# Fourth queries with third values, fourth keys with fourth values: a regrouping of paired products in a streaming-encoder block

## The chip, the cores and the metric

The kernel runs on one core of a Trainium2 chip. The metric is device time in microseconds of one execution, the median of several runs. PE is the engine of matrix products, PEld its weight loads, DVE the vector engine, ACT the scalar engine, POOL the general engine and SP the queue that issues most transfers.

## What is computed

One layer of a block with two parallel branches, in float32, for 256 positions and a model width of 4096 (the reference, cut):

```python
xn = rms_norm(h, norm_in_g)
proj = xn @ w_in                      # 4096 x 14336
q, k, v, z_a, a_c, g_c, z_c = split(proj, 7 parts of 2048)
y_a = chunked_attention(q, k, v, rel_table)          # 16 heads of 128
y_a = rms_norm(y_a, attn_out_g) * silu(z_a)
y_c = conv_module(a_c, g_c, ...)  # a * sigmoid(g), 31-tap causal conv, layer norm, swish, @ w_pw
y_c = rms_norm(y_c, conv_out_g) * silu(z_c)
h = h + concat([y_a, y_c]) @ w_out
h = h + sigmoid(rms_norm(h) @ w_ple_gate + b) * (p @ w_ple)
out = rms_norm(h, final_g)
```

The change touches the part from `proj` to the layer norm of the convolution branch.

## The kernel before

**Exact products from parts.** Every float32 operand is split into a high and a low part: ACT copies the high part (`wh`, line 204), DVE subtracts it to get the low part (`wl`, line 205). A block product is three matmuls of 128x512 (high x high, low x high, high x low). The tags `wh` and `wl` have three tiles each, so the split can run at most three parts ahead of PE.

**Pairs of columns.** `mixed_product` multiplies x with two column blocks of 512 at once, for both halves of the 256 positions. It walks over 16 pairs of 128-row blocks in the order of a list. A plain pair does four block products for each of its two row blocks, 24 matmuls in all. A marked pair (`*` or `+`) does seven block products instead of eight, so 21 matmuls, at the price of sums of weight blocks: for `*` DVE makes four of them (lines 465, 466, 472, 473), for `+` two come ready from memory through an accumulating transfer issued on POOL (line 419) and DVE makes the other two. The sums are split as well (`uh`, `ul`). The combinations of x that a marked pair needs (`xS`) exist for pairs 0, 2, 4 and 6 from the start; for 8 and 10 they are made by `more_combinations` during one group.

Marked pairs need four more accumulators, the helpers P1, P5, P7 and P6. They take all four tiles of the pool of temporary PSUM banks (`ps_tmp`) from the first marked pair of a group to its last; attention, transposes and the matmuls of the layer norm use the same four banks at other times. After the last marked pair `on_helpers` reads them out.

A single product (`product`, line 229) has no marked pairs: 192 matmuls for one column block.

**Fills.** DVE work that is due later waits in the list `later`; after each pair of a group a few items are taken from it (`fill`, with counts such as `early_fills`). Items are the 124 taps of each of the four convolution groups (lines 717 and 721) and the 71 steps of `layer_norm_swish`: sums and mean (9 with pauses), centering and squares (20), variance, pauses, spread, pauses (10), 16 swishes and 16 splits into `uS`. The order on the engines is then settled by a scheduler that may move a ready instruction ahead of one that has to wait.

**Memory.** `upool` holds the sums of weights and their parts and some combinations of x; it is closed (`first_sums.close()`) when no marked pair of this part is left, and `more`, the pool of `uS`, is opened in its place. The tag `hd` has five tiles, for uT, biases, transposed keys, values, and the sum and squares of the layer norm.

**The order of groups** is written out by hand: convolution group 0 and 1; queries and keys 0; values 0 and 1 as a pair; attention 0; convolution group 2; queries and keys 1; attention 1; convolution group 3; queries and keys 2; values 2 alone; attention 2; layer norm put in the list; queries and keys 3, with `norm_fills`; `more` opened; values 3 alone; attention 3; then the pointwise product, which reads `uS`.

Of the kernel before, what the change touches and what calls it, by code (L numbers as in the profile page):

```python
# [10 lines left out]
F32 = mybir.dt.float32  # L11
F32R = mybir.dt.float32r
AF = mybir.ActivationFunctionType
# [3 lines left out]
P = 128  # L17
NB = 512
# [7 lines left out]
def hybrid_block(  # L26
# [23 lines left out]
    nc = tc.nc  # L50
# [131 lines left out]
    def fill(n):  # L182
        for _ in range(min(n, len(later))):
            later.popleft()()
# [139 lines left out]
    def units(text):  # L324

        return [(int(u.rstrip("*+")), u[-1] if u[-1] in "*+" else "") for u in text.split()]
# [2 lines left out]
    dense = units("1 0* 3 2* 5 4* 6* 7 8* 9 10* 11 12* 14* 13 15")  # L329
    first = units("0 1 3 5 7 9 11 13 15 2* 8 4* 10 6* 12 14")  # L330
    early = units("1 3 5 0+ 7 9 2+ 11 13 4+ 15 8 6+ 10 12 14")
    early_six = units("1 3 5 0+ 7 2* 9 4+ 11 6* 13 8+ 15 10* 12 14")

    early_fills = (5, 6, 1, 5, 6, 1, 5, 6, 1, 5, 6, 1, 2, 5, 5, 4)
    six_fills = (6, 6, 1, 5, 1, 5, 1, 5, 1, 5, 1, 5, 1, 6, 7, 7)
    norm_fills = (5, 5, 2, 5, 5, 2, 5, 5, 2, 5, 5, 2, 2, 4, 5, 5)
    final = units("1 0* 3 2* 5 4* 6* 7 8* 9 10* 12* 11 13 14 15")
    late = units("1 3 5 7 9 11 13 15 0* 2 4* 6 8* 10* 12 14")

    def mixed_product(  # L340
        w, col, lhs, comb, order, on_helpers, ahead=None, fills=(0,), on_begin=None, apart=NB,
        left=(), begin=None,
    ):


# [81 lines left out]
        for n, (pair, seven) in enumerate(order):  # L427
            if n < done:
                continue
            if ahead:  # L430
                ahead(pair)
            wts = []
            for k in range(2):
                wt = wpool.tile([P, 2, NB], F32, tag="w", name="wt")
                if seven == "+" and k == 0:
                    nc.sync.dma_start(wt[:, 0], w[2 * pair * P : (2 * pair + 1) * P, col : col + NB])
                else:
                    nc.sync.dma_start(wt, two_columns(w, 2 * pair + k, col, apart))
                wts.append(wt)
            sums_ahead(n)  # L440
            if n >= len(order) - n_left:
                for k in range(2):
                    tiles = left[2 * (n - len(order) + n_left) + k]
                    held.append((2 * pair + k, parts_of(wts[k], 2, tiles and tiles())[0]))
                fill(fills[n % len(fills)])
                continue
            if not seven:
                for k in range(2):
                    add_plain(n, k, *parts_of(wts[k], 2)[0])
                fill(fills[n % len(fills)])  # L450
                continue
            begins = not helper
            if begins:
                for name in ("P1", "P5", "P7", "P6"):
                    helper[name] = ps_tmp.tile([P, NB], F32, tag="tmp", name=f"acc_{name}")
                banks.update(helper)
            w0, w1 = wts
            plus = partial(nc.vector.tensor_tensor, op=ALU.add)
            before = list(recent)
            w0h, w0l = parts_of(w0, 1)[0]  # L460
            if seven == "+":
                ua = ub = sums[n]
            else:
                ua = ub = upool.tile([P, 2, NB], F32, tag="u", name="ua")
                plus(ua[:, 0], w0[:, 0], w0[:, 1])  # L465
                plus(ua[:, 1], w0[:, 1], w1[:, 1])  # L466
            with queued_behind(before if seven == "+" else ()):
                uah, ual = pair_parts(ua)
            w1h, w1l = parts_of(w1, 2)[0]
            if seven == "*" and not sums:  # L470
                ub = upool.tile([P, 2, NB], F32, tag="u", name="ub")
            plus(ub[:, 0], ua[:, 0], w1[:, 1])
            plus(ub[:, 1], ub[:, 0], w1[:, 0])  # L473
            ubh, ubl = pair_parts(ub)
            first = len(made)

            def s_of(i):
                t, at = comb[pair] if isinstance(comb, dict) else (comb[pair // 4], pair % 4)
                return [t[:, at + i // 2, q, (i % 2) * P : (i % 2 + 1) * P] for q in range(2)]

            k0, k1 = 2 * pair, 2 * pair + 1
            add("P1", block(k0, 0), (w0h[:, 0], w0l[:, 0]), n, True)
            add("P5", s_of(1), (uah[:, 0], ual[:, 0]), n, True)
            add("P7", s_of(0), (uah[:, 1], ual[:, 1]), n, True)
            add("P2", block(k1, 0), (w1h[:, 0], w1l[:, 0]), n, True)
            add("P3", s_of(3), (w1h[:, 1], w1l[:, 1]), n, True)
            add("P6", s_of(2), (ubh[:, 0], ubl[:, 0]), n, True)
            add("P4", block(k1, 1), (ubh[:, 1], ubl[:, 1]), n, True)
            if begins and on_begin:
                on_begin()  # L490
            if begins:
                tc.add_manual_dep(
                    made[first].ins, last_transpose[0].ins.name,
                    mybir.DependencyInfo(mybir.DependencyClass.NoSync, mybir.DependencyReason.DATA),
                    reason="transposes before the helpers take their banks",
                )
            if n == last_seven:
                on_helpers(helper)
            fill(fills[n % len(fills)])
        after.close()  # L500
        return (c, add_left) if left else c
# [10 lines left out]
        tt(z[1][0], helper["P7"], z[1][0], ALU.add)  # L512
        tt(z[1][1], helper["P5"], z[1][0], ALU.add)

    def sum_tiles(**kw):

        kw = kw or dict(tag="stage")
        t = [spool.tile([P, NH, NB], F32, name="z", **kw) for _ in range(2)]
        return t, [[t[j][:, h] for j in range(2)] for h in range(NH)]

    def scaled_pair(w, col, apart, order, r, fills, home={}, **kw):

        t, z = [], []

        def on_helpers(helper):
            for dst, src in zip((t, z), sum_tiles(**home)):
                dst.extend(src)
            nc.scalar.activation(z[0][0], helper["P1"], AF.Identity, scale=r[:, :1])
            helper_sums(helper, z)
            for h, j in QUARTERS[1:]:  # L530
                nc.scalar.activation(z[h][j], z[h][j], AF.Identity, scale=r[:, h : h + 1])

        c = mixed_product(w, col, xT, xS, order, on_helpers, fills=fills, apart=apart, **kw)
        for h, j in QUARTERS:
            stt(
                z[h][j], c[h][j], r[:, h : h + 1], z[h][j],
                ALU.mult, ALU.subtract if j else ALU.add,
            )
        return t
# [193 lines left out]
    def glu_conv(c):  # L733
        if c == 0:
            sg, gate = scaled_pair(
                w_in0, o_a, o_g - o_a, first, r_x, (1,), begin=first_pairs
            )
        else:
            last = c == CW // NB - 1
            sg, gate = scaled_pair(  # L740
                w_in0, o_a + c * NB, o_g - o_a, *((early_six, r_x, six_fills) if last else (early, r_x, early_fills)),
                ahead=more_combinations if last else None,
            )
        for h in range(NH):
            nc.scalar.activation(gate[:, h, :], gate[:, h, :], AF.Sigmoid)
# [193 lines left out]
        )  # L939
        nc.gpsimd.memset(bias[: P // 2, :, : P // 2], NEG)  # L940

    def keys(g, fills):
        q, k = scaled_pair(w_in0, o_q + g * NB, o_k - o_q, early, r_x, fills)
        qs[g] = act.tile([P, GH, T], F32, tag="act", name="qT")
        to_heads(q, qs[g])
        ks[g] = hd_tile("kT")
        to_heads(k, ks[g])

    def paired_values(g, order, fills, **kw):
        vs[g], vs[g + 1] = scaled_pair(w_in0, o_v + g * NB, NB, order, r_x, fills, **kw)  # L950

    def single_values(g):
        accv = product(w_in0, o_v + g * NB, xT, KD)
        vs[g] = spool.tile([P, NH, NB], F32, tag="hd", name="v", bufs=5)
        for h in range(NH):
            nc.scalar.activation(vs[g][:, h, :], accv[h], AF.Identity, scale=r_x[:, h : h + 1])

    n_g = H // GH
    assert n_g == CW // NB == 4
    glu_conv(0)  # L960
    glu_conv(1)
    load_bias(0)
    keys(0, early_fills)
    paired_values(0, early, early_fills, home=dict(tag="hd", bufs=5))
    attention(0)
    glu_conv(2)
    load_bias(1)
    keys(1, early_fills)
    attention(1)
    glu_conv(3)  # L970
    load_bias(2)
    keys(2, early_fills)
    single_values(2)
    attention(2)
    layer_norm_swish()
    load_bias(3)
    keys(3, norm_fills)
    first_sums.close()
    more = pool("more", 4)
    single_values(3)  # L980
    attention(3)
    r_a = rstd_of(ssq_a, AW, "r_a")

# [22 lines left out]
    for c0, order in zip(range(0, CW // NB, 2), point):  # L1006
# [7 lines left out]
        def on_helpers(helper):  # L1014
            y_tiles()
            z.extend([ys[j][:, h, :] for j in range(2)] for h in range(NH))
            tt(z[0][0], helper["P1"], rows[0], ALU.add)
            helper_sums(helper, z)
            for h, j in QUARTERS[1:]:
                tt(z[h][j], z[h][j], rows[j], ALU.subtract if j else ALU.add)  # L1020
# [318 lines left out]
```

## Time and profile before

| what | value |
|---|---|
| median of 3 runs | 2033.08 us (2032.29 to 2034.44) |
| the profiled execution | 2032.83 us |
| its span, first to last instruction | 2031.1 us |
| PE, DVE, ACT busy | 99%, 92%, 59% |
| granted TensorE clock | 0.998 |

A group row of the profile gives the line, the engine, the tiles written and read, the count, then busy time, the mean time of one in ns, and the idle time just before with what ended it. A row of the windows view gives a stretch, its length, and for each engine the busy time and the number of instructions, then the granted clock, the DMA engines' busy share and GB/s. Matmul durations overlap, so the spacing of matmuls is read from starts or from long runs, not from the duration of one.

### The profile page before, as it was taken

The page shows a single profiled execution, that of the slowest core. Times are in us where ns is not written, and L with a number is a line of the kernel's source. Part 1 is how long each engine was busy: PE and PEld are TensorE (multiplying, and loading weights), DVE is VectorE, ACT ScalarE, POOL GpSimd, SP SyncE. Part 2 cuts the span into 40 slices and gives each one's busy share as a digit, 9 for nine tenths or more (in the row PEclk, how much of TensorE's full clock was granted, in tenths as well). Part 3 has the DMA queues.
Part 4 walks back from the last instruction along what each step waited for, and adds up shares of the span by engine and source line. Part 5 has one row for each costly group of instructions (what it writes and reads, how often), then busy time and mean ns, then how long its engine had stood idle before and what let it go on. Part 6 is the DMA issues. An engine that isn't in the chain of part 4 may idle for free.

```text
span 2031.1 us, 26144 instructions
## 1 busy us (share of the span) xinstructions
PE 2015.5 (99%) x9094; PEld 1658.7 (82%) x9094; DVE 1871.1 (92%) x2658; ACT 1203.3 (59%) x1568; POOL 46.0 (2%) x50
## 2 busy tenths in 40 slices
PE   9999999999999999999999999999999999999997
PEld 7888888888888888888888888888888888888876
DVE  7999999679999986868899999999999999999998
ACT  7655555655655445676556566675665666665555
POOL 0000000000000000000000000000000000000000
PEclk9999999999999999999999999999999999999999
DMA  8787878688678867556666666676666656666765
GB/s 294 223 237 233 257 214 251 191 245 239 188 217 250 254 187 207 171 185 205 194 214 198 202 205 214 217 229 209 206 213 201 208 187 207 204 220 205 234 208 179
DMA packets 171167, 436.69 MB, mean 215 GB/s; under 512 B 13966, under 2 KB 17182, under 8 KB 171034
## 3 DMA queue, kind: packets, MB, share of 16 engines
q1 hardware_dynamic: 161952, 417.93, 64.0%
q0 software_dynamic: 8432, 16.25, 4.9%
q8 instruction: 71, 1.16, 0.2%
q10 hardware_dynamic: 650, 0.84, 0.1%
q14 instruction: 62, 0.51, 0.1%
HBM read 430.77 MB, written 4.19 MB: 214 GB/s over the span
## 4 chain that ended last, share of the span: by engine, by line
PE 92%; DVE 5%; issue 2%; ACT 1%; DMA 1%; POOLq 0%; POOL 0%; ACTq 0%; DVEq 0%
PE acc L383 67%; PE acc_P L383 16%; PE acc L229 5%; DVE wl L205 2%; PE tmp_ps L170 1%; DVE cv L721 1%; DMA wt<-in_w_out_dram 0%; PE tmp_ps L890 0%; DVE ul L205 0%; PE tmp_ps L874 0%; PE tmp_ps L908 0%; PE tmp_ps L913 0%; ACT wh L204 0%; PE acc L371 0%; DVE cv L799 0%
## 5 line engine op out<-in xcount | busy, mean ns | idle before, releaser
L383 PE MATMUL acc<-wh,big_t 128*128 128x512 f32 x3992 | 1234.7, 391 | 0.7 <-DVE y_c L1030 0.3
L204 ACT CAST wh<-wt 128x1024 fp32r<-128x1024 f32 (+1 forms) x737 | 713.4, 978 | 550.5 <-PE acc L383 365.0
L205 DVE TENSOR_TENSOR wl<-wt,wh 128x1024 fp32r<-128x1024 f32 (+1 forms) x737 | 821.8, 1127 | 82.0 <-ACT wh L204 78.6
L383 PEld LDWEIGHTS acc<-wh,big_t 128*128 128x128 f32 x3992 | 746.8, 188 | 155.1 <-issue 0.9
L383 PE MATMUL acc<-wl,big_t 128*128 128x512 f32 x1996 | 770.7, 391 | 0.6 <-DVE wl L205 0.5
L383 PEld LDWEIGHTS acc<-wl,big_t 128*128 128x128 f32 x1996 | 374.3, 188 | 79.5 <-DVE wl L205 2.3
L204 ACT CAST uh<-ua 128x1024 fp32r<-128x1024 f32 x160 | 168.3, 1052 | 80.9 <-DVE ua L466 46.1
L721 DVE SCALAR_TENSOR_TENSOR cv<-uT,dw,cv 128x250 f32<-128x250 f32 (+19 forms) x480 | 202.3, 463 | 1.1
L205 DVE TENSOR_TENSOR ul<-ua,uh 128x1024 fp32r<-128x1024 f32 x160 | 194.9, 1218 | 8.4 <-ACT uh L204 8.0
L383 PE MATMUL acc_P<-uh,big_t 128*128 128x512 f32 x516 | 157.9, 391 | 0.0
L204 ACT CAST uh<-ub 128x1024 fp32r<-128x1024 f32 x92 | 96.8, 1053 | 95.8 <-DVE ub L473 86.5
L205 DVE TENSOR_TENSOR ul<-ub,uh 128x1024 fp32r<-128x1024 f32 x92 | 112.2, 1220 | 6.1 <-ACT uh L204 5.2
L383 PEld LDWEIGHTS acc_P<-uh,big_t 128*128 128x128 f32 x516 | 95.8, 188 | 22.3 <-ACT uh L204 3.1
L383 PE MATMUL acc_P<-ul,big_t 128*128 128x512 f32 x258 | 98.8, 391 | 0.1
L229 PE MATMUL acc<-wh,big_t 128*128 128x512 f32 x304 | 93.9, 390 | 0.0
L465 DVE TENSOR_TENSOR ua<-wt 128x512 f32<-128x512 f32 x95 | 65.1, 685 | 18.3 <-DMA wt<-in_w_in_dram 12.4
L383 PE MATMUL acc<-uh,big_t 128*128 128x512 f32 x252 | 78.1, 390 | 0.0
L383 PE MATMUL acc_P<-wh,big_t 128*128 128x512 f32 x252 | 77.8, 389 | 0.0
L229 PEld LDWEIGHTS acc<-wh,big_t 128*128 128x128 f32 x304 | 56.9, 188 | 11.9 <-issue 0.2
L383 PE MATMUL acc_P<-uh,comb_t 128*128 128x512 f32 x216 | 66.4, 390 | 0.1
L466 DVE TENSOR_TENSOR ua<-wt 128x512 f32<-128x512 f32 x95 | 64.9, 683 | 1.1 <-DMA wt<-in_w_in_dram 1.1
L473 DVE TENSOR_TENSOR ub<-ub,wt 128x512 f32<-128x512 f32 x92 | 63.0, 685 | 0.8
(250 smaller groups left out, 1589.3 us busy)
## 6 DMA issues: line engine op xcount, KB each, us to landing
wt<-in_w_in_dram SPq DMA_DIRECT2D x416, 512.0 KB, 4.5
wt<-in_w_out_dram SPq DMA_DIRECT2D x128, 512.0 KB, 4.3
wt<-in_w_ple_gate_dram SPq DMA_DIRECT2D x128, 512.0 KB, 4.2
wt<-in_w_pw_dram SPq DMA_DIRECT2D x32, 512.0 KB, 4.7
ua<-in_w_in_dram SPq DMA_DIRECT2D x31, 512.0 KB, 4.2
ua<-in_w_in_dram POOLq DMA_DIRECT2D x31, 512.0 KB, 8.3
wt<-in_w_in_dram SPq DMA_DIRECT2D x31, 256.0 KB, 2.7
hc<-in_x_dram SPq DMA_DIRECT2D x8, 512.0 KB, 4.8
```

Of the source, the lines that this page charges most:

```text
L170: nc.tensor.transpose(pt[:, i * T + h * P : i * T + (h + 1) * P], src[:, h, b] if len(src.shape) == 4 else src[:, h, b * P : (b + 1) * P], ...
L204: nc.scalar.copy(wh[:, :kc, :], wt[:, :kc, :]),
L205: nc.vector.tensor_tensor(wl[:, :kc, :], wt[:, :kc, :], wh[:, :kc, :].bitcast(F32), ALU.subtract),
L229: nc.tensor.matmul(acc, a, b[:, k, :], start=kb == 0 and kind == 0, stop=kb == kblocks - 1 and kind == 2,)
L383: nc.tensor.matmul(banks[name], a, b, start=name not in begun, stop=final and ends[name] == n and kind == 2 and not (left and name in "P2 ...
L465: plus(ua[:, 0], w0[:, 0], w0[:, 1])
L466: plus(ua[:, 1], w0[:, 1], w1[:, 1])
L473: plus(ub[:, 1], ub[:, 0], w1[:, 0])
L721: nc.vector.scalar_tensor_tensor(cv[:, i, PAD - k :], uT[:, i, : T + k - PAD], dw[:, b, k : k + 1], cv[:, i, PAD - k :], ALU.mult, ALU.add,)
```

## The change

Four things change.

- Convolution group 2 gets the order with six marked pairs, as group 3 has; the two further combinations of x are made in group 2 instead of group 3.
- Queries 3 and values 2 become a pair (five marked pairs), ahead of attention 2; keys 3 and values 3 become a pair (four marked pairs), ahead of attention 3. No single product is left here.
- The last of these groups has an order of its own: six plain pairs first, the marked ones after them. Its fills sum to 71, the whole layer norm.
- `upool` is closed and `more` opened after the last marked pair of that group, in its middle, through a new hook `after_sevens`; the 16 splits follow in the fills of the three plain pairs left.

```diff
+    early_five = units("1 3 5 0+ 7 9 2+ 11 4* 13 6+ 15 8* 10 12 14")
...
-    norm_fills = (5, 5, 2, 5, 5, 2, 5, 5, 2, 5, 5, 2, 2, 4, 5, 5)
+    norm = units("1 3 5 7 9 11 0+ 13 2* 15 4+ 8 6* 10 12 14")
+    norm_fills = (7, 8, 8, 8, 6, 4, 2, 3, 2, 3, 2, 2, 0, 6, 5, 5)
...
             if n == last_seven:
                 on_helpers(helper)
+                after_sevens()
...
-    def sum_tiles(**kw):
-
-        kw = kw or dict(tag="stage")
-        t = [spool.tile([P, NH, NB], F32, name="z", **kw) for _ in range(2)]
+    def sum_tiles(*homes):
+
+        homes = homes or (dict(tag="stage"),) * 2
+        t = [spool.tile([P, NH, NB], F32, name="z", **kw) for kw in homes]
...
-            last = c == CW // NB - 1
             sg, gate = scaled_pair(
-                w_in0, o_a + c * NB, o_g - o_a, *((early_six, r_x, six_fills) if last else (early, r_x, early_fills)),
-                ahead=more_combinations if last else None,
+                w_in0, o_a + c * NB, o_g - o_a,
+                *((early, r_x, early_fills) if c == 1 else (early_six, r_x, six_fills)),
+                ahead=more_combinations if c == 2 else None,
             )
...
+    def heads(*parts, order=None, fills=early_fills, **kw):
+
+        cols = [o + g * NB for o, g in parts]
+        tiles = scaled_pair(
+            w_in0, cols[0], cols[1] - cols[0], order or early, r_x, fills,
+            homes=[home if o == o_v else dict(tag="stage") for o, _ in parts], **kw
+        )
+        for (o, g), t in zip(parts, tiles):
+            if o == o_v:
+                vs[g] = t
+            else:
+                (queries_of if o == o_q else keys_of)(g, t)
+
+    def open_late():
+
+        nonlocal more
+        first_sums.close()
+        more = pool("more", 4)
...
     glu_conv(3)
     load_bias(2)
-    keys(2, early_fills)
-    single_values(2)
+    heads((o_q, 2), (o_k, 2))
+    heads((o_q, 3), (o_v, 2), order=early_five)
     attention(2)
     layer_norm_swish()
     load_bias(3)
-    keys(3, norm_fills)
-    first_sums.close()
-    more = pool("more", 4)
-    single_values(3)
+    heads((o_k, 3), (o_v, 3), order=norm, fills=norm_fills, after_sevens=open_late)
     attention(3)
```

More of the change, by code (lines that the diff above doesn't have):

```diff
@@ L341, in mixed_product @@
         w, col, lhs, comb, order, on_helpers, ahead=None, fills=(0,), on_begin=None, apart=NB,
-        left=(), begin=None,
+        left=(), begin=None, after_sevens=lambda: None,
     ):
@@ L513, in helper_sums, with scaled_pair @@
         tt(z[1][1], helper["P5"], z[1][0], ALU.add)
-    def sum_tiles(**kw):
-        kw = kw or dict(tag="stage")
-        t = [spool.tile([P, NH, NB], F32, name="z", **kw) for _ in range(2)]
+    def sum_tiles(*homes):
+        homes = homes or (dict(tag="stage"),) * 2
+        t = [spool.tile([P, NH, NB], F32, name="z", **kw) for kw in homes]
         return t, [[t[j][:, h] for j in range(2)] for h in range(NH)]
-    def scaled_pair(w, col, apart, order, r, fills, home={}, **kw):
+    def scaled_pair(w, col, apart, order, r, fills, homes=(), **kw):
         t, z = [], []
         def on_helpers(helper):
-            for dst, src in zip((t, z), sum_tiles(**home)):
+            for dst, src in zip((t, z), sum_tiles(*homes)):
                 dst.extend(src)
@@ L940, in load_bias, with queries_of, keys_of @@
         nc.gpsimd.memset(bias[: P // 2, :, : P // 2], NEG)
-    def keys(g, fills):
-        q, k = scaled_pair(w_in0, o_q + g * NB, o_k - o_q, early, r_x, fills)
+    home = dict(tag="hd", bufs=5)
+    def queries_of(g, st):
         qs[g] = act.tile([P, GH, T], F32, tag="act", name="qT")
-        to_heads(q, qs[g])
+        to_heads(st, qs[g])
+    def keys_of(g, st):
         ks[g] = hd_tile("kT")
[L947 to L956, printed above, removed]
+        to_heads(st, ks[g])
+    def heads(*parts, order=None, fills=early_fills, **kw):
[13 more added lines that the diff above has]
+        more = pool("more", 4)
     n_g = H // GH
@@ L962, in hybrid_block @@
     load_bias(0)
-    keys(0, early_fills)
-    paired_values(0, early, early_fills, home=dict(tag="hd", bufs=5))
+    heads((o_q, 0), (o_k, 0))
+    heads((o_v, 0), (o_v, 1))
     attention(0)
@@ L967, in hybrid_block @@
     load_bias(1)
-    keys(1, early_fills)
+    heads((o_q, 1), (o_k, 1))
     attention(1)
```

## The prediction

> **What bounds the kernel now.** I read the page first, then who waited for whom on PE, then the windows of the stages that the change touches.
>
> ```profile
> span 2031.1 us, 26144 instructions
> PE 2015.5 (99%) x9094; PEld 1658.7 (82%) x9094; DVE 1871.1 (92%) x2658; ACT 1203.3 (59%) x1568; POOL 46.0 (2%) x50
> PE 92%; DVE 5%; issue 2%; ACT 1%; DMA 1%; POOLq 0%; POOL 0%; ACTq 0%; DVEq 0%
> PE acc L383 <- DVE wl L205: 0.5, 1, 0.5
> PE acc L383 <- DVE y_c L1030: 0.3, 1, 0.3
> ```
>
> The third line is the chain that ended last: it runs on PE. The last two are PE's waits (total, times, longest): apart from the start they are the longest in 2031 us. So PE's own stream sets the time, and a matmul taken out is worth its spacing, as long as nobody comes late in its place. The next view is the windows, cut where the groups' first matmuls start: third convolution group (with attention 0), fourth (attention 1), third queries and keys, third values, fourth queries and keys (attention 2), fourth values.
>
> ```profile
> core 0: us, PE busy (x) PEld busy (x) DVE busy (x) ACT busy (x) POOL busy (x), PEclk, DMA share, GB/s
> 356.45:447.87 91.42, 91.42 (x422) 75.13 (x421) 60.08 (x76) 52.17 (x79) 4.87 (x4) 1.00 0.75 219
> 534.47:625.77 91.30, 91.30 (x428) 75.09 (x425) 87.76 (x144) 56.94 (x89) 3.65 (x3) 1.00 0.70 205
> 625.77:713.00 87.23, 87.11 (x396) 72.14 (x395) 87.18 (x143) 47.70 (x53) 5.17 (x5) 1.00 0.82 241
> 713.00:757.17 44.17, 44.17 (x200) 36.61 (x198) 36.90 (x60) 17.86 (x19) 0.00 (x0) 1.00 0.65 195
> 757.17:850.20 93.03, 92.50 (x424) 75.12 (x423) 69.96 (x98) 56.75 (x85) 2.74 (x3) 1.00 0.64 190
> 850.21:896.90 46.69, 46.69 (x220) 39.15 (x220) 37.65 (x68) 34.52 (x58) 0.72 (x1) 1.00 0.62 192
> ```
>
> PE is full in all six, at full granted clock. DVE is also full in the fourth row (87.18 of 87.23), yet has 31 us idle in the first and 23 us in the fifth. Why, the convolution taps of line 721 show, in the windows view of that line alone (DVE busy and count):
>
> ```profile
> 356.45:447.87 91.42, 0.00 (x0) 1.00 0.75 219
> 625.77:713.00 87.23, 32.93 (x78) 1.00 0.82 241
> 713.00:757.17 44.17, 17.61 (x42) 1.00 0.65 195
> ```
>
> The taps are filler. A group takes about 80 of them although its fills name 64, and a group that finds none left is idle. DVE at 100% is thus no proof that DVE limits that group.
>
> **Matmuls removed.** A plain pair issues 2 x 4 x 3 = 24 matmuls, a marked one 7 x 3 = 21, a single product 2 x 3 x 32 = 192. The third convolution group goes from 4 marks to 6: 372 becomes 366. Before, the four groups of third and fourth queries, keys and values issue 372 + 192 + 372 + 192 = 1128; after, 372 + 369 (five marks) + 372 (four) = 1113. Together 21 fewer. The spacing comes from the chain's pieces:
>
> ```profile
> 713.29 43.57 PE acc L229 x192
> 853.63 1.75 PE tmp_ps L874 x16
> ```
>
> 43.57 / 192 = 0.227 us, so 21 x 0.227 = **-4.76 us**. The 32 transposes of queries and keys stay 32 (16, 8 and 8 instead of 16 and 16; 0.11 us each), and attention and layer norm keep theirs.
>
> The Trainium skill (TensorE: Matmul & The Clock Gate, "Back-to-back issue gap") gives about 131 ns for each 512-column matmul in a sustained stream with weight loads; by that 21 would be worth 2.75 us. The row above says 227 and decides.
>
> **The stall that goes.** PE's one wait among these groups lies where helper sums, centering and squares met:
>
> ```profile
> 838.51 1.98 PE L383 MATMUL acc<-wh,big_t 128*128 128x512 f32 x8
> 841.01 1.20 PE L383 MATMUL acc<-wl,big_t 128*128 128x512 f32 x4 [0.53 <-DVE wl L205]
> ```
>
> Eight matmuls from 838.51 at 0.227 end their slots at 840.33; the next starts at 841.01: 0.68 us lost. In the new order centering and squares precede the first marked pair. I take -0.68.
>
> **DVE's added work, and what hides it.** Prices (min/median/max, or mean of one):
>
> ```profile
> L205 DVE TENSOR_TENSOR wl<-wt,wh x48: 683/1220/1227, 759.6 to 894.8; 128x1024 fp32r<-128x1024 f32 x44, 128x512 fp32r<-128x512 f32 x4
> L205 DVE TENSOR_TENSOR ul<-ua,uh 128x1024 fp32r<-128x1024 f32 x160 | 194.9, 1218 | 8.4 <-ACT uh L204 8.0
> L466 DVE TENSOR_TENSOR ua<-wt 128x512 f32<-128x512 f32 x95 | 64.9, 683 | 1.1 <-DMA wt<-in_w_in_dram 1.1
> ```
>
> Plain pair: 2 x 1.22 = 2.44. A "+" pair: 0.68 + 1.22 + 2 x 1.22 + 2 x 0.68 (lines 472, 473) = 5.70. A "*" pair adds lines 465 and 466: 7.06.
>
> - *Third convolution group.* Two "+" and two plain become four "*": 28.2 - 11.4 - 4.9 = +11.9, and two combinations of x (5 us at most) move in from the fourth group: 60.1 + 16.9 = 77 of 91.42 - 1.36 = 90.1. The idle time hides it: 0. The fourth group ran this very order with 87.76 busy, and PE waited for nothing.
> - *Fourth queries with third values.* The old window of third queries and keys (87.18) with 42 taps instead of 78 (-15.3), one more mark (+3.3) and two "*" (+2.7): 77.9 of 86.5. Cost 0; the cover is 8.6 us.
> - *Fourth keys with fourth values.* To 69.96 come two "*" (2.7) and what moves in from the next window, whose groups are (busy, mean):
>
> ```profile
> L844 DVE TENSOR_TENSOR big_t<-cv,big_t 128x256 fp32r<-128x256 f32 x16 | 5.7, 415 | 0.0
> L832 DVE TENSOR_TENSOR cv<-cv,rs 128x256 f32<-128x256 f32 x16 | 5.6, 417 | 0.0
> L535 DVE SCALAR_TENSOR_TENSOR z<-acc,r_x,z 128x512 f32<-128x512 f32 x4 | 3.0, 743 | 0.0
> L833 ACT ACTIVATE cv<-cv,prm 128x256 f32<-128x256 f32 x16 | 8.5, 592 | 0.0
> L843 ACT CAST big_t<-cv 128x256 fp32r<-128x256 f32 x16 | 5.3, 404 | 0.0
> DVE wl L205 <- ACT wh L204: 24.9, 20, 2.9
> ```
>
> That is 69.96 + 2.7 + 5.7 + 5.6 + 3.0 = 87 of some 92 us; ACT gets 56.8 + 13.8 = 71. The last row is DVE's wait over both windows: DVE waits for ACT's half of a part, held back by the three part buffers, which is slack and can be filled. Still, 5 us is thin cover.
>
> **The statistics.** Mean, variance and spread each need one of four temporary banks; the helpers hold all four from the first marked pair to the last.
>
> ```profile
> L787 PE MATMUL tmp_ps<-lnsum,mean_w x2: 379/431/483, 829.8 to 830.1; 128*128 128x256 f32 x2
> L803 ACT ACTIVATE sq<-cv x4: 1047/1062/1064, 833.3 to 844.3; 128x1024 f32<-128x1024 f32 x4
> L782 ACT ACTIVATE rs<-tmp_ps x1: 385/385/385, 853.7 to 853.7; 128x256 f32<-128x256 f32 x1
> L889 PE MATMUL tmp_ps<-kT,qT x8: 270/275/275, 756.7 to 775.5; 128*128 128x128 f32 x8
> L915 PE MATMUL tmp_ps<-v,pT x8: 275/275/275, 763.6 to 780.3; 128*128 128x128 f32 x8
> 780.68 0.62 PE L383 MATMUL acc_P<-wh,big_t 128*128 128x512 f32 x2
> ```
>
> So before, they came only after the helpers, at 829.8. The new order puts six plain pairs first: 6 x 24 x 0.227 = 32.7 us, plus attention 2's share of PE (756.7 to 780.68 holds three plain pairs, 16.3, so 7.6 are its own), eight transposes (0.9) and the statistics' matmuls (about 1): the first marked pair is due 42 us after the group starts. The chain from mean to the scaled spread took 853.7 + 0.4 - 829.8 = 24.3 us. Started after the first pair (8 us in), it ends at 32. But a first square needs one of five "hd" tiles, all taken (bias, keys, values of attention 2, the next bias, the sum) until attention 2 nears its end, some 20 us in; from first square to the end is 854.1 - 833.3 = 20.8, with helper sums in between that are gone now: 41 at most, against 42. The unknown is worth 0 to 2 us; I take 0.3, near the lower end, because DVE has most centering done while it waits.
>
> On POOL, the power of the variance now stands near the first "+" pair's DMA and the bias memset; behind a "+" DMA it would wait, and the chain with it; POOL has long gaps, so 0. SP's weight loads pass only the bias load, as before.
>
> **The late pool.** Its tiles take the place of the helper scratch, so the first split waits for the last marked pair's matmuls. ACT is in order: behind that split stand the casts of the next pairs. ACT already waits there for the helper copies, and three plain pairs (16.3 us) cover 5.3 us of casts and 5.7 of splits. I allow 0.4, the size of the stall at 841 and less. Attention 3 now follows its own keys' transposes directly, as attention 1 does before, without a PE wait: 0.
>
> **Sum**: -4.76 - 0.68 + 0.3 + 0.4 = -4.7. The profiled execution took 2032.83 (span 2031.1), 0.25 under the median of 2033.08; so 2028.1 for it and **2028.4** for the median. Its own range is 2027.6 (no new stall) to 2029.4. A measurement of this kernel tells about 0.2%, 4.1 us, from no change, so the forecast stands just on the faster side.
>
> **Rivals.**
>
> *Statistics late.* Mean gets its bank only when attention 2 ends, 780.3 - 756.7 = 23.6 us in: 23.6 + 24.3 = 47.9 against 42, 5.7 late; PE can run at most 12 matmuls of the next pair ahead (2.7). Stall 3.0 to 5.7, net -2.4 to +0.3: 2030.7 to 2033.4, likeliest 2032. For it: the bank shortage is what held mean back until 829.8. Against: each head takes three temporary tiles one after the other, not four at once. Chance 0.20.
>
> *DVE becomes the bound* in the group of fourth keys and values; this is slower. If the idle time there (93.03 - 69.96 = 23.1) can't be filled because the order of the queue leaves it, DVE needs 87 + 23.1 = 110 for 92: 18 late, less the three part buffers' lead (36 matmuls, 8.2): 9.9 late, net +4.5, and 2037.6. With half filled, 6.5 late, the lead covers it; it decides when nearly nothing is filled. For it: 1 of 20 waits there already reached PE. Against: full DVE without PE waits at 625.77. The Trainium skill (Perfetto Trace Analysis, "Identifying the Most-Contended Engine") counts occupancy as a fair measure for Vector and would work on the fullest such engine first; DVE's 92% would speak against more marks, but of the fullest window above 32.93 of 87.18 are taps, which move. Chance 0.16.
>
> *Freed matmuls cost less than their spacing*: if the weight load sets the pace (1658.7 / 9094 = 0.182 us), 21 are worth 3.8, with nothing else changed 2029.3. Against: 0.227 in 192 in a row. By the skill's figure above it would be 2.75, and 2030.3. Chance 0.02.
>
> *The third convolution group gets nothing from its marks*, because the combinations of x wait for tiles or for DVE behind attention 0: 1.36 is lost again and about 0.5 more, 2030.3. Against: the fourth did the same without a wait. Chance 0.06.
>
> **From these to the numbers.** Forecast 0.56 (faster); late statistics, slower spacing and lost marks 0.28 (within 0.2%); DVE bound 0.16 (slower). The range reaches from 2026.8 (the lower end, less the 0.8 us by which single runs stand under the median) to 2035.5, which takes in the middle cases and the milder part of the slower one.
>
> **What would show it.** Right: 21 fewer matmuls on PE; windows of 366, 369 and 372 matmuls at 0.227 plus small ones; statistics done before the first helper matmul of the last group; no PE wait over 1 us from 356 us on. Wrong: a PE wait on the spread or a temporary bank before that helper; PE waits on "wl" or "ul" in the last group (DVE bound); a gap at the first matmul of the pointwise product, if the splits come late.

## The result, and the profile after

| | before | after |
|---|---|---|
| median of 13 runs each | 2033.36 us (2032.29 to 2034.44) | 2029.11 us (2027.82 to 2030.91) |
| ratio, 95% interval | | 0.9979 [0.9971, 0.9987] |
| the profiled execution | 2032.83 us | 2028.23 us |
| granted clock | 0.998 | 0.998 |

4.25 us less, forecast 4.7. The profiled executions stand 4.60 apart, and these are read here. First the page of the changed kernel and who waited for whom on PE (total, times, longest); `L385` is the matmul that was L383 before.

```profile
span 2026.5 us, 26195 instructions
PE 2010.8 (99%) x9073; PEld 1654.4 (82%) x9073; DVE 1903.4 (94%) x2708; ACT 1215.0 (60%) x1583; POOL 46.9 (2%) x50
PE acc L385 <- DVE y_c L1043: 0.4, 1, 0.4
PE acc_P L385 <- DVE ul L205: 0.4, 2, 0.2
PE tmp_ps L830 <- DVE lnsum L829: 0.2, 1, 0.2
```

21 matmuls fewer (9094 - 9073), DVE 32 us busier, and apart from the start no wait of PE longer than 0.4 us. The windows of the changed kernel are cut near the first matmuls of the same groups: third convolution group; fourth; third queries and keys; fourth queries with third values; fourth keys with fourth values; start of the pointwise product.

```profile
core 0: us, PE busy (x) PEld busy (x) DVE busy (x) ACT busy (x) POOL busy (x), PEclk, DMA share, GB/s
356.60:446.66 90.06, 90.06 (x416) 74.07 (x415) 73.46 (x101) 54.76 (x83) 3.65 (x3) 1.00 0.70 212
533.27:624.52 91.25, 91.25 (x428) 75.27 (x426) 84.19 (x132) 56.44 (x87) 3.66 (x3) 1.00 0.70 210
624.52:711.12 86.60, 86.58 (x391) 71.50 (x390) 86.55 (x143) 46.61 (x52) 5.18 (x5) 1.00 0.82 238
711.12:796.40 85.28, 85.28 (x386) 70.80 (x385) 80.10 (x112) 45.63 (x52) 3.95 (x4) 1.00 0.77 231
796.40:892.14 95.74, 95.12 (x444) 77.12 (x443) 82.95 (x138) 71.45 (x120) 1.63 (x1) 1.00 0.54 169
892.14:942.39 50.25, 50.20 (x241) 40.46 (x240) 42.83 (x79) 32.73 (x60) 1.06 (x1) 1.00 0.58 191
```

The whole gain lies between the first and the last cut. Before, that stretch ran from 356.45 to 896.90 (540.45); now from 356.60 to 892.14 (535.54): -4.91. Not all of this is gain: the first four matmuls of attention 3 stand ahead of the last cut before, and behind it now (one row of each):

```profile
896.49 0.38 PE L889 MATMUL tmp_ps<-kT,qT 128*128 128x128 f32 x2
```

```profile
892.91 0.49 PE L892 MATMUL tmp_ps<-kT,qT 128*128 128x128 f32 x2
```

Before, the next matmul starts at 896.95, so they take 0.46 us, and like for like the stretch became about 4.5 us shorter, of the 4.60. Within it, the third convolution group gives 91.42 - 90.06 = 1.36 in these two profiles. The tail from the third queries and keys to the pointwise product took 896.90 - 625.77 = 271.13 and takes 892.14 - 624.52 = 267.62: -3.51, again with those 0.46.

The chain that ended last, in the last group of the changed kernel (start, length, what), shows the statistics:

```profile
817.24 0.22 PE tmp_ps L918 x2
817.47 0.43 PE tmp_ps L790 x2
...
828.27 5.96 PE acc L385 x25
...
836.75 0.27 DVE lnsum L829
...
838.15 0.71 DVE cv L835 x2
...
842.41 1.15 DVE ul L205
843.56 0.04 issue
843.60 0.50 PE acc_P L385
...
874.49 16.81 PE acc L385 x74
```

L918 is the last matmul of attention 2, L790 the mean, L829 the scaling before the spread, L835 the first multiplication with it. The mean comes right behind attention 2, 817.47 - 796.40 = 21.07 us into the group. PE then meets the chain at three places, where a row of DVE stands among its own: before 828.27, at the spread (836.96 on PE) and before 843.60. By the starts of the matmuls around them, PE loses 0.42, 0.39 and 0.51 us there over the spacing of 0.227, 1.3 us in all. The first matmul on a helper starts at 838.9, 0.7 us after the first multiplication with the spread. The last row is the three plain pairs at the end: one piece without a gap.

### The profile page after: what moved, and what is told of

It reads as the page before. It is cut to its first block, busy times and chain, and to the rows that moved or that the text cites. A ratio compares the mean times of both kernels' runs of the same rounds, so it can differ in the third digit from the quotient of the medians.

```text
span 2026.5 us, 26195 instructions
## 1 busy us (share of the span) xinstructions
PE 2010.8 (99%) x9073; PEld 1654.4 (82%) x9073; DVE 1903.4 (94%) x2708; ACT 1215.0 (60%) x1583; POOL 46.9 (2%) x50
## 4 chain that ended last, share of the span: by engine, by line
PE 95%; DVE 3%; issue 1%; ACT 1%; DMA 0%; POOLq 0%; POOL 0%; ACTq 0%; SPq 0%; DVEq 0%
PE acc L385 73%; PE acc_P L385 17%; PE tmp_ps L170 1%; DVE cv L724 1%; PE acc L229 1%; DVE wl L205 1%; PE tmp_ps L893 0%; PE tmp_ps L877 0%; PE tmp_ps L911 0%; PE tmp_ps L916 0%; PE acc L373 0%; ACT wh L204 0%; PE tmp_ps L892 0%; DVE ul L205 0%; DMA xin<-in_x_dram 0%
## 5 line engine op out<-in xcount | busy, mean ns | idle before, releaser
L385 PE MATMUL acc<-wh,big_t 128*128 128x512 f32 x4154 | 1283.3, 391 | 0.6 <-DVE y_c L1043 0.4
L385 PEld LDWEIGHTS acc<-wh,big_t 128*128 128x128 f32 x4154 | 777.0, 188 | 160.8 <-DVE y_c L1043 0.9
L385 PE MATMUL acc<-wl,big_t 128*128 128x512 f32 x2077 | 801.9, 391 | 0.1
L385 PEld LDWEIGHTS acc<-wl,big_t 128*128 128x128 f32 x2077 | 389.5, 188 | 82.5 <-DVE wl L205 1.8
L204 ACT CAST uh<-ua 128x1024 fp32r<-128x1024 f32 x174 | 182.9, 1052 | 91.1 <-DVE ua L468 46.3
L205 DVE TENSOR_TENSOR ul<-ua,uh 128x1024 fp32r<-128x1024 f32 x174 | 212.0, 1219 | 9.6 <-ACT uh L204 8.1
L385 PE MATMUL acc_P<-uh,big_t 128*128 128x512 f32 x528 | 161.8, 392 | 0.0
L385 PEld LDWEIGHTS acc_P<-uh,big_t 128*128 128x128 f32 x528 | 98.0, 188 | 23.2 <-ACT uh L204 3.7
L385 PE MATMUL acc_P<-ul,big_t 128*128 128x512 f32 x264 | 101.3, 392 | 0.0
L467 DVE TENSOR_TENSOR ua<-wt 128x512 f32<-128x512 f32 x102 | 69.9, 685 | 17.3 <-DMA wt<-in_w_in_dram 10.7
L385 PE MATMUL acc<-uh,big_t 128*128 128x512 f32 x266 | 82.5, 390 | 0.0
L385 PE MATMUL acc_P<-wh,big_t 128*128 128x512 f32 x266 | 82.1, 389 | 0.0
L468 DVE TENSOR_TENSOR ua<-wt 128x512 f32<-128x512 f32 x102 | 69.6, 683 | 4.3 <-DMA wt<-in_w_in_dram 3.6
L385 PE MATMUL acc_P<-uh,comb_t 128*128 128x512 f32 x228 | 70.1, 390 | 0.1
L474 DVE TENSOR_TENSOR ub<-ua,wt 128x512 f32<-128x512 f32 x92 | 62.9, 683 | 0.3
L385 PEld LDWEIGHTS acc_P<-ul,big_t 128*128 128x128 f32 x264 | 49.3, 188 | 12.5 <-DVE ul L205 2.0
```

What stands on the lines that cost most here:

```text
L204: nc.scalar.copy(wh[:, :kc, :], wt[:, :kc, :]),
L205: nc.vector.tensor_tensor(wl[:, :kc, :], wt[:, :kc, :], wh[:, :kc, :].bitcast(F32), ALU.subtract),
L385: nc.tensor.matmul(banks[name], a, b, start=name not in begun, stop=final and ends[name] == n and kind == 2 and not (left and name in "P2 ...
```

## Experiments

The kernel before ran beside each on the same chip, and its time is given. Except for e7 and e9 to e11, each is one execution, and a run of the changed kernel on the same chip is on record only beside e9 and e10; so these experiments are read from the rows of the groups concerned, and less from the times. The rivals tested were: the statistics' place in the group; DVE as the bound; the late pool; the third convolution group; and whether the marks' gain goes on.

**e1: where the marked pairs stand in the last group.** The old mixed order and fills instead of `norm`.

```diff
-    heads((o_k, 3), (o_v, 3), order=norm, fills=norm_fills, after_sevens=open_late)
+    old_fills = (5, 5, 2, 5, 5, 2, 5, 5, 2, 5, 5, 2, 2, 4, 5, 5)
+    heads((o_k, 3), (o_v, 3), fills=old_fills, after_sevens=open_late)
```

> The last group in the old order (marks from the fourth pair on) with the old fills; the same 21 matmuls fewer than before. If the place of the marks is what lets the layer norm fit, the mean comes only after the helpers are read (about 66 us into the group), and mean to spread (20.8 us), swishes (some 15) and splits (some 10) then run past the group's end: PE waits at the pointwise product, and the execution takes 2040 to 2060 us. If the order does not matter, and only the count of matmuls does, it stays within 2 us of 2028.

Measured: 2037.34 us (before beside it 2032.62). PE's longest wait, and the chain of this group around the spread:

```profile
PE acc L385 <- ACT wh L204: 2.6, 1, 2.6
```

```profile
820.39 0.43 PE tmp_ps L790 x2
...
871.53 0.60 PE tmp_ps L817 x4
...
873.60 0.70 PE tmp_ps L830 x4
...
876.95 4.54 ACT cv L836 x9
...
884.23 2.06 ACT cv L836 x4
886.29 0.94 ACT wh L204
...
887.27 10.06 PE acc L385 x36
```

The mean (L790) comes as early as in the changed kernel, which the expectation had otherwise. It is the variance (L817) that gets its bank only behind the helpers, though its squares are done by 838 us, and so the spread comes some 35 us later in its group than in the changed kernel. The swish activations (L836) then stand in one block on ACT ahead of a weight part's cast, and PE waits for that cast. By the starts of the groups' first matmuls, the last group lasts 98.90 us (changed kernel: 95.26), and the first 22 us of the pointwise product grow by 3.2. So the order, with the fills that go with it, is worth some 7 us: the time missed the 2040 to 2060 expected, but without this order the regrouping is slower than before in this run.

**e2: the mean ahead of attention 2.**

```diff
-    attention(2)
     layer_norm_swish()
+    fill(9)
+    attention(2)
...
-    norm_fills = (7, 8, 8, 8, 6, 4, 2, 3, 2, 3, 2, 2, 0, 6, 5, 5)
+    norm_fills = (6, 6, 7, 7, 4, 2, 2, 3, 2, 3, 2, 2, 0, 6, 5, 5)
```

> The first nine steps of the layer norm (sums, mean) are issued ahead of attention 2, so the mean asks for its bank first; later fills are nine smaller in sum. If the mean was held back by its place behind attention 2, it now comes within 5 us of the group's start, the spread comes 3 to 10 us earlier against the first marked pair, and the wait of 0.4 us on it is gone: time 0 to 1 us under the changed kernel. If the squares' tiles (held by attention 2) set the chain, the mean comes early and the spread does not move by more than 2 us.

Measured: 2027.47 us (before 2032.62). Two lines of the code in its trace (min/median/max in ns, first and last start), and its last group from first product matmul to the next group's, here and then in the changed kernel:

```profile
L790 PE MATMUL tmp_ps<-lnsum,mean_w x2: 379/380/382, 796.5 to 796.7; 128*128 128x256 f32 x2
L830 PE MATMUL tmp_ps<-lnsum,mean_w x4: 275/275/311, 829.7 to 830.0; 128*128 128x128 f32 x4
```

```profile
797.39:890.38 92.99, 92.99 (x439) 76.74 (x437) 83.05 (x140) 70.07 (x118) 1.63 (x1) 1.00 0.56 175
```

```profile
796.88:892.14 95.26, 94.64 (x440) 76.67 (x439) 82.47 (x137) 70.97 (x119) 1.63 (x1) 1.00 0.55 170
```

PE is busy in every instant of the group, and the spread comes at 829.7 instead of 837.0. None of the three places in the chain above is left, so they did come from the statistics. But the group ahead of it is 0.46 us longer here (the mean stands there now), and the pointwise product takes about 1.1 us back:

```profile
PE acc L385 <- DVE y_c L1042: 0.6, 2, 0.3
PE acc L385 <- DVE y_c L1044: 0.3, 1, 0.3
```

**e4: the pool opened after the group** instead of within it.

```diff
-    heads((o_k, 3), (o_v, 3), order=norm, fills=norm_fills, after_sevens=open_late)
+    heads((o_k, 3), (o_v, 3), order=norm, fills=norm_fills[:13] + (0, 0, 0))
+    open_late()
```

> The late pool is opened after the last group instead of within it, and the 16 splits come after the group's fills. If opening it within the group matters, the pointwise product waits for the first splits: a PE gap of 2 to 8 us at its first matmul, 2030 to 2036 us. If the scheduler pulls the splits forward anyway, the time stays within 1 us of 2028.

Measured: 2029.21 us (before 2032.62). The splits on DVE:

```profile
L847 DVE TENSOR_TENSOR big_t<-cv,big_t x16: 415/418/420, 878.4 to 888.3; 128x256 fp32r<-128x256 f32 x16
```

In the changed kernel they run from 875.9 to 887.3. They still run within the group though they are issued after it, because the scheduler moves them forward. Opening the pool early costs nothing and brings nothing that one run can show. What the splits would cost behind the group was therefore not tested.

**e5: DVE's room in the last group.** Sixteen more 128x256 operations, one behind each multiplication with the spread, which change no value.

```diff
             nc.vector.tensor_tensor(cv[:, i, :], cv[:, i, :], st["rs"], ALU.mult)
+            nc.vector.scalar_tensor_tensor(cv[:, i, :], cv[:, i, :], 0.0, cv[:, i, :], ALU.mult, ALU.add)
```

> Sixteen further operations on DVE of 128x256 (about 0.39 us each, 6.2 us together), one behind each swish product; they leave the values as they are. If DVE bounds the marked part of the last group, PE waits grow by nearly all of it, 5 to 6 us: 2033 to 2035 us. If the part buffers' lead and DVE's idle time cover it, as the forecast says, PE waits grow by 0 to 2 us: 2028 to 2030 us.

Measured: 2033.68 us (before 2032.62), span 2031.9: 5.4 us over the changed kernel's. The added operations took 6.4 us of DVE's time (mean 418 ns each, a little overlapped) and not 6.2. PE's waits in this kernel, the four parts of the changed kernel's last group, and the third of them here:

```profile
PE acc L385 <- ACT wh L204: 1.9, 2, 1.3
PE acc L385 <- DVE wl L205: 1.7, 2, 1.4
```

```profile
796.40:817.47 21.07, 21.07 (x114) 16.83 (x113) 11.93 (x27) 14.81 (x35) 0.00 (x0) 1.00 0.45 128
817.47:838.90 21.43, 21.05 (x96) 16.94 (x96) 19.74 (x35) 14.15 (x21) 1.63 (x1) 1.00 0.49 157
838.90:875.90 37.00, 36.76 (x161) 29.85 (x160) 35.15 (x49) 30.52 (x44) 0.00 (x0) 1.00 0.61 191
875.90:892.14 16.24, 16.24 (x77) 13.50 (x77) 16.13 (x30) 11.96 (x24) 0.00 (x0) 1.00 0.59 189
```

```profile
838.90:875.90 37.00, 36.76 (x159) 29.10 (x158) 37.00 (x61) 30.02 (x40) 0.00 (x0) 1.00 0.54 169
```

Then this kernel's last group, from first product matmul to the next group's, and the first 22 us of the pointwise product, here and in the changed kernel:

```profile
797.10:895.23 98.13, 95.63 (x434) 75.51 (x433) 85.46 (x151) 70.78 (x119) 1.64 (x1) 1.00 0.51 159
895.23:919.49 24.26, 22.35 (x118) 17.65 (x119) 17.38 (x40) 16.41 (x37) 0.00 (x0) 1.00 0.43 146
```

```profile
892.14:913.82 21.68, 21.63 (x115) 16.80 (x114) 15.23 (x38) 15.87 (x37) 0.00 (x0) 1.00 0.41 138
```

DVE's idle 12.8 us of the changed kernel's last group lie mostly ahead of the mean: 21.07 - 11.93 = 9.1. From the mean on it is busy for 71.02 of 74.67 us. Between the first helper matmul and the splits 1.85 us were left (37.00 - 35.15), and the added work filled them. The rest arrived at PE later: 98.13 - 95.26 = 2.9 us in the group, mostly in its last plain pairs, and 24.26 - 21.68 = 2.6 us in the pointwise product.

**e8: the same sixteen operations one group earlier**, beside taps of the fourth convolution group.

```diff
+            if b == 15 and k < 16 and k != PAD:
+                nc.vector.scalar_tensor_tensor(cv[:, i, :], cv[:, i, :], 0.0, cv[:, i, :], ALU.mult, ALU.add)
```

> The same 16 added 128x256 vector operations as in e5 (0.39 us each, 6.2 us in all, they change no value), but beside sixteen of the last taps of the fourth convolution group, in the group of fourth queries and third values, where DVE was busy 80.1 of 85.3 us. Theory A (what counts is the place: in the last group nothing is left to put off, here the taps can slide): +0 to +1 us against the changed kernel, 2029 to 2030. Theory B (VectorE's total load sets the pace from the third convolution group on): +4 to +6 us, as in e5, 2033 to 2035.

Measured: 2031.09 us (before 2034.1). Fourth queries with third values, from first product matmul to the next group's, here and then in the changed kernel:

```profile
713.36:798.87 85.51, 85.18 (x384) 70.38 (x382) 84.69 (x128) 45.63 (x52) 3.95 (x4) 1.00 0.79 231
```

```profile
712.01:796.88 84.87, 84.87 (x384) 70.43 (x382) 79.69 (x112) 45.22 (x51) 3.95 (x4) 1.00 0.78 232
```

DVE takes in 5.0 us more and the group grows by 0.64; the last group lasts 95.21 us against 95.26, so nothing is added there. What counts is the place, not DVE's total. The time itself fits neither theory's range, but of the 2.8 us by which this span exceeds the changed kernel's, 1.35 lie ahead of the group and 0.9 behind the last cut, where the added operations have no part.

**e3: fewer taps** (the third and fourth convolution groups keep one tap each).

```diff
-            for k in reversed(range(TAPS)):
+            for k in reversed(range(TAPS)) if c < 2 else (PAD,):
```

> Leaves out 30 of the 31 taps of the third and fourth convolution groups, so 240 vector operations of some 0.32 us (about 77 us of VectorE's time between 533 and 796 us) are gone, and the output is not the reference's. The layer norm's steps keep their place behind attention 2. Theory A (the taps are filler, pulled forward into idle time, and VectorE is not the bound of those groups although it shows 78 to 100% there): the time stays within 1 us of the changed kernel's 2029, whatever DVE's share falls to; DVE in the window 624 to 711 falls from 86.6 to some 60 us. Theory B (the change is limited by VectorE's load in the groups that got the marks): the stretch from 533 to 796 gets shorter by 3 us or more, and the time falls to 2026 or below.

Measured: 2030.60 us (before 2034.1). Third queries and keys, and fourth queries with third values:

```profile
625.00:711.70 86.70, 86.70 (x393) 71.82 (x391) 59.96 (x66) 46.68 (x52) 5.17 (x5) 1.00 0.82 241
711.70:797.00 85.30, 85.30 (x386) 70.84 (x385) 65.03 (x69) 45.60 (x51) 3.95 (x4) 1.00 0.78 231
```

DVE falls from 86.55 to 59.96 in the first, and both groups are as long as in the changed kernel (86.60 and 85.28). The full DVE there was filler. The time is 1.6 us over the 2029 expected, a little more than theory A allowed; it didn't fall, as theory B wanted.

**e6: four marks again in the third convolution group.**

```diff
-                *((early, r_x, early_fills) if c == 1 else (early_six, r_x, six_fills)),
-                ahead=more_combinations if c == 2 else None,
+                *((early, r_x, early_fills) if c < 3 else (early_six, r_x, six_fills)),
+                ahead=more_combinations if c == 3 else None,
```

> Puts the third convolution group back to four marked pairs (the two extra combinations are made in the fourth group, as before the change) and keeps the new pairing of queries, keys and values. Six matmuls more than the changed kernel. Theory A (the gain is removed matmuls at the windows' own 0.227 us, and third group's DVE has room): 6 x 0.227 = +1.4 us, the third group's length goes back from 90.06 to 91.4, time near 2030.5. Theory B (the third group's marks are free or cost something through DVE): within 0.3 us of the changed kernel.

Measured: 2032.39 us (before 2034.1), with this window between the same cuts as above:

```profile
357.44:448.86 91.42, 91.42 (x422) 75.13 (x421) 60.14 (x76) 52.20 (x79) 4.87 (x4) 1.00 0.75 219
```

91.42 with 422 instructions against 90.06 with 416: six matmuls are 1.36 us, 0.227 each, in both directions. The single run's time, 1.7 us under before, is too scattered to add to that. But this gain doesn't come whole in every execution. In the ten profiles of kernels that leave this group as the change made it, it lasts 89.86 to 91.23 us, in the middle 90.5; the longest is e1's:

```profile
356.98:448.21 91.23, 90.76 (x417) 73.92 (x415) 73.61 (x101) 54.69 (x83) 3.65 (x3) 1.00 0.70 210
```

In the long ones PE waits for `wl` within a marked pair (0.47 us at 424.7 in e1), though DVE is idle for over 17 of the 91 us. Why it waits in some executions and not in others stays open.

**e7: more marks.** The two further combinations of x are made in convolution group 1, five marks stand in the four pairs of heads that had four (one of the four edits is shown), and the mean comes ahead of attention 2.

```diff
-                ahead=more_combinations if c == 2 else None,
+                ahead=more_combinations if c == 1 else None,
...
-    heads((o_q, 1), (o_k, 1))
+    heads((o_q, 1), (o_k, 1), order=early_five)
```

> A version that goes on in the change's direction: six and five marks in the earlier groups too (two more combinations already in the second convolution group, five marks in queries/keys 0 to 2 and the two first values), 12 matmuls fewer than the changed kernel, and the layer norm's mean ahead of attention 2 as in e2. Theory A (each matmul removed is worth 0.227 us as long as VectorE's taps can move): 2029.1 - 12 x 0.227 - 0.8 = 2025.6. Theory B (VectorE is at its edge in those groups, which are at 84 to 100% busy): the pairs' combinations take the place of taps that then fall due later, in the last groups, and the time is 2028 to 2034.

Measured: 2033.05 us (before 2034.1), ratio 0.9995 [0.9986, 1.0004]: 12 matmuls fewer, and the gain of the change is gone. Second queries and keys, from first product matmul to the next group's, in this kernel, then in the changed one:

```profile
448.22:535.03 86.81, 86.79 (x388) 70.51 (x387) 86.35 (x135) 47.95 (x54) 3.96 (x4) 1.00 0.76 227
```

```profile
446.66:533.27 86.61, 86.56 (x392) 71.51 (x390) 86.56 (x143) 46.62 (x52) 5.17 (x5) 1.00 0.82 238
```

Three matmuls fewer in as much time: what 0.68 us less PE work should have brought went in part into waits of a tenth of a microsecond or two. The third convolution group waited too, in its window (90.06 us in the changed kernel, with DVE 73.46 busy) and in PE's waits:

```profile
356.71:448.22 91.51, 90.72 (x416) 73.83 (x415) 87.61 (x142) 54.76 (x83) 3.65 (x3) 1.00 0.68 204
```

```profile
PE acc L385 <- DVE wl L205: 0.8, 2, 0.5
```

Cut the same way, the first two values are 0.9 us shorter, the first and the third queries and keys 0.7 and 0.5 longer, each with three matmuls fewer. So the fifth mark pays in the pair of values and in none of the three pairs of queries and keys; why isn't settled. Another 2.6 us lie behind the last cut, where the mean ahead of attention 2 costs about 1.1 (as in e2); the rest is in code that is the same in all these kernels.

**e11, e10, e9: the changed kernel and the mean's place in more rounds on one chip.** e10 is e2's kernel; e9 puts the mean behind the first head of attention 2 (`attention(2, lambda: fill(9))`).

> The changed kernel itself once more, as the base for the two runs beside it on the same chip: 4 to 4.5 us under the kernel before (ratio 0.998), as in its first run, by both theories.

> The kernel of e2 (the layer norm's mean ahead of attention 2) in more rounds. Theory A (the three stalls at the statistics, about 1.1 us, and 1.2 us more of the last group can go, of which the start of the pointwise product gives about 1 us back): 0.8 to 1.7 us under the changed kernel on this chip. Theory B (e2's one profile was within the scatter of single runs): within 0.4 us of it.

> As e2, but the mean's matmul comes after the first head of attention 2 and not ahead of it. Theory A (in e2 the mean ahead of the attention cost 0.4 us at the handover from the group of fourth queries, 1.77 us between the two groups' matmuls against 1.35, because PE met the mean before VectorE had folded the sum): 0.3 to 0.4 us under e2. Theory B (the handover is long because PE's mean takes its own time): no change to e2 (within 0.2 us).

| kernel | median | ratio to before (2033.62) |
|---|---|---|
| e11, the changed kernel | 2029.10 us | 0.9980 [0.9971, 0.9988] |
| e10, mean ahead of attention 2 | 2028.99 us | 0.9976 [0.9967, 0.9986] |
| e9, mean behind its first head | 2028.72 us | 0.9978 [0.9969, 0.9987] |

The change's own gain repeats. The three can't be told apart: e2's 0.8 us in one profile is not shown to be a gain of the time.

e11 also shows how far one execution can be trusted. Its profiled one took 2032.47 us, 4.2 more than the first profile of the same kernel, yet from the third convolution group to the pointwise product (535.54 us there) it is nearly as long:

```profile
358.05:893.76 535.71, 534.95 (x2445) 440.15 (x2444) 493.87 (x762) 321.27 (x439) 23.24 (x21) 1.00 0.72 215
```

Of the rest, 1.4 us lie in the first 102 us and 2.6 behind the last cut.

## Why the prediction was right

- **Matmuls removed, -4.76.** Right in count and in price. e6 shows 6 of the 21 at 0.227 by themselves, though part of that is lost again to waits in some executions. The Trainium skill (TensorE: Matmul & The Clock Gate, "Back-to-back issue gap") gives about 131 ns for one, and an estimate from that would have been 0.79 us for those six; the measured 1.36 decides.
- **The stall that goes, -0.68, and the statistics, +0.3.** The first was right, the second was too small, and its premise was wrong. The 0.68 before the old L383 matmul is gone. The statistics cost 1.3 instead of 0.3: the three places at 828, 837 and 843, which are gone in e2. The mean didn't start 8 us in: it came at 21.07, right behind attention 2, as the rival of late statistics had it. It cost little because the chain from mean to scaled spread took 838.15 - 817.47 = 20.7 us (mean to first multiplication with the spread) instead of the 24.3 taken from before, where four helper sums of 0.68 us each (L510 to L513) stood on DVE within it. 21.1 + 20.7 = 41.8 against the 42 at which the marks were due. So the rival's premise was right and its price wrong, since it took the chain's length from a trace in which the chain shared DVE with the helpers. That the chain ended in time, by less than 1 us, is luck as far as the start of the mean goes; the other bound of the forecast, 41 us at most by way of the squares, came out nearly right. Two of the signs named against the forecast did show, both small: PE waited for the spread and for `ul`.
- **DVE's added work, 0.** The busy times came out near (73.46 for 77, 80.10 for 77.9, 82.95 for 87), and PE waited little. The 77 had an error in it: the order with six marks has three "*" and three "+", so at the forecast's prices +10.6 and not +11.9. Nor was the third convolution group's cost always 0: the ten profiles counted at e6 lose up to 1.2 us there. But the reason given for the last group fell. I called the 24.9 us of DVE's waits for ACT slack that can be filled, and the cover 5 us. e5 shows that hardly any was left behind the spread: 2.9 + 2.6 = 5.5 of 6.4 us came through. The idle time is there, ahead of the mean, where the layer norm's work can't go. The rival of DVE as the bound thus described the group's state rightly (idle that the order leaves), and stayed harmless because the work fits into what remains, with 0.9 us (6.4 - 5.5) to 1.9 us to spare.
- **The late pool, +0.4.** The trace puts it at nothing: the three plain pairs run without a gap (874.49, 16.81 us in one piece), and e4's last group, whose splits stand up to 1.7 us later in it, is as long (95.24 us).
- **The rest of the tail.** 15 matmuls are 3.40 of its 3.51, and the 0.46 of attention 3 only move across the cut. Counted by the matmuls' starts, PE's waits at the products grew by 0.8 (the three new stalls and some small ones, less the old one), and the 32 transposes, which the forecast left equal, take 0.5 less (3.7 before, 3.25 now). Why the transposes gain isn't shown.
- **The third convolution group without a gain** didn't come true: all ten profiles are shorter than the 91.42 of before, by 0.2 to 1.6 us. Full DVE as a sign of a bound is ruled out by e3 for the two groups shown there; e7 shows that more work put into such groups isn't free.

The median came out 0.7 us above the forecast, within its own range (2027.6 to 2029.4). The main term carried it. That the rest came out so near is in part luck: statistics 1.0 dearer, against the late pool 0.4 and the transposes 0.5 cheaper.

## What to carry to other kernels

Price a removed matmul by its spacing in a long run of the same stream, and ask for each added vector operation in which stretch it must run: the same sixteen operations cost 0.64 us in one group and 5.5 from the next one on. A full vector engine says nothing until the movable work has been taken out of it, and an idle one nothing until it is known on which side of the next dependency the idle time lies. Put a chain of small steps that need a shared bank ahead of the work that holds the bank: here that order, with its fills, was worth some 7 us in one run, more than the gain of the regrouping.

## What the runs showed that I had not expected

A group with fewer matmuls isn't always shorter though PE is 99% busy: in e7, three matmuls fewer took 86.81 us instead of 86.61. The power of the variance on POOL took 1.63 us here (the POOL column of the last group), that of attention's norm 1.06 us in the following window; both are 128x2.
